# Decode beside a dense layer: a third key buffer, gathers one step ahead, and products of keys tied to the dense products

## The chip, the cores and the metric

One core of a Trainium2 chip runs the kernel in one launch. The metric is the device time of that launch in microseconds (us); the median of several runs counts. TensorE (PE) multiplies matrices, VectorE (DVE) and ScalarE (ACT) work on rows, GpSimd (POOL) gathers by index and does small operations, SyncE (SP) issues loads and stores.

## The reference

One layer of a decoder for a prompt of 512 tokens and, in the same launch, one new token for each of 8 sequences that have 4096 past tokens each. Both go through the same weights; the new tokens also read paged caches of keys and values (32 pages of 128 tokens, 8 heads of 64).

```python
h = rmsnorm(x, g_pre_mix)
qf, kf, vf, logf, qg, kg, vg, la, og, gfox, ggla = split(h @ w_in)
o_fox = softmax(q k^T / 8 + decay of the log forget gates, causal) @ v      # prompt
# new tokens, for each of 8 sequences:
lp = einsum('bqhd,bkhd->bhqk', q, k_past) * scale + suffix_sums(logf_past) + cn
ln = q . k_new * scale
p  = softmax over [lp, ln];  o_fox = p @ [v_past, v_new]
S_new, o_gla = gla(state, qg, kg, vg, la)                                   # chunks of 64
u = sigmoid(gfox) * (o_fox @ w_fox_out) + sigmoid(ggla) * (o_gla @ w_gla_out)
x = x + rmsnorm(u @ w_o)
x = x + rmsnorm(square(relu(rmsnorm(x) @ w_up)) @ w_down)
```

## The kernel before

**Dense work.** Everything is float32. A weight is loaded in pieces of 128x2x256 (`raw`, L234, on SP's queue) and split into a high part `wh` (a cast on ScalarE, L222) and a low part `wl` (a subtraction on VectorE, L223); the activations `h` and `c` are split likewise. A product of 256 columns is then three products per 128 rows of depth: high by high, high by low, low by high. Every product goes through the helper `mm` (L85), so its line is L85 whatever it computes; tiles tell them apart: `pmm` is dense work, `pdv` the value products of decode, `px` and `pd` smaller ones. The order in the code is: queries, the forget gates (`gates_small`: L372 to L379, a polynomial of ten steps on VectorE whose results are `lfs` for the new tokens and `lft` for the prompt; `lft` is transposed at L419), keys and values, the GLA projections, the output gates, the mix, w_o (`wo_fin` at L1181, once for each of four blocks of 128 rows: a sum of squares, a reciprocal root on GpSimd at L218, the residual sum at L1185, transposes at L324, and the split of the new `h` at L327 and L223), then the MLP.

**Decode.** `decode()` (L549) is a generator of steps (b, g): sequence b, group g of 16. `pump` (L643) is called between dense products and runs one step for every 3.1 us of dense work that has been written. A step gathers pages with `page_load` (L209, on GpSimd): `kk`, 512 KB of keys, 16 for a sequence, and `kv`, 1 MB of values, 8 for a sequence. `kk` and `kv` have two buffers each. A step multiplies keys by the query (L574) and reduces over the head (L575), both on VectorE, each in place or into `sc`. After the 16th step come the maximum (`mx`, L604 to L607), a transpose (L610), the common maximum (`dm`, L612 and L613), and the exponentials. While sequence b does its keys, TensorE multiplies the values of sequence b-1 (four `pdv` products for each `kv`).

**What sets the order.** The program is written in one order in Python; a scheduler that simulates a timeline then places each engine's instructions, by dependencies, buffers and the written order. Each engine runs its own list strictly in that order. A gather into `kk` waits for the reduction that last read its buffer, and one into `kv` for the last product that read it.

## Time and profile before

| | |
|---|---|
| median of three runs | 1068.25 us (1065.61 to 1074.95) |
| profiled execution | 1071.62 us |
| its span | 1069.9 us |
| mean granted TensorE clock | 0.956 |
| TensorE busy | 996.6 us, 93% |
| VectorE busy | 690.2 us, 65% |
| ScalarE busy | 427.3 us, 40% |
| GpSimd busy | 270.0 us, 25% |

The span is what the profiler saw, and the profiled execution is a run of its own beside the three. Busy time counts work, not waits; a TensorE that runs at half its clock counts as busy too, so its busy time is to be read with the granted clock. Decode runs from about 24 to 776 us of the span.

### The profile page before, as it was taken

What the parts mean: (1) busy time and instruction counts of PE and PEld (TensorE: products, weight loads), DVE (VectorE), ACT (ScalarE), POOL (GpSimd) and SP (SyncE); (2) the same over time, 40 slices, a digit from 0 to 9 for tenths busy, and PEclk for the clock granted to TensorE, in tenths of its full rate; (3) what the DMA queues carried; (4) which work ended last, traced back from release to release, by engine and by line L of the source; (5) the groups of instructions that cost most, each with busy time, mean ns of one, the idle gap of its engine ahead of it and who ended that gap; (6) DMA issues with size and microseconds to landing.
All of it is one profiled execution on the core that took longest, in us unless ns stands there. A gap on an engine that the chain in (4) does not pass through costs nothing.

```text
span 1069.9 us, 20743 instructions
## 1 busy us (share of the span) xinstructions
PE 996.6 (93%) x8183; PEld 830.5 (78%) x8183; DVE 690.2 (65%) x1238; ACT 427.3 (40%) x1110; POOL 270.0 (25%) x256
## 2 busy tenths in 40 slices
PE   7998999999999899999894799999999799999996
PEld 5987867867977787797784678788787588888995
DVE  8577766867989858887669779567333333233356
ACT  6424544534833414333233444336313453115442
POOL 5232243353342313423334333430100000000001
PEclk9997999999999979999896899999999899999999
DMA  6746788587578638966994687994667366677222
GB/s 194 251 143 197 272 299 286 182 314 276 169 284 292 190 103 266 310 222 205 343 346 154 232 318 240 330 335 142 222 229 237 120 205 214 213 237 235 81 76 86
DMA packets 134279, 242.03 MB, mean 226 GB/s; under 512 B 11627, under 2 KB 105150, under 8 KB 125990
## 3 DMA queue, kind: packets, MB, share of 16 engines
q0 software_dynamic: 28032, 135.28, 36.0%
q1 hardware_dynamic: 106150, 105.43, 31.0%
q8 instruction: 64, 1.05, 0.4%
q14 instruction: 33, 0.27, 0.1%
HBM read 235.14 MB, written 5.47 MB: 225 GB/s over the span
## 4 chain that ended last, share of the span: by engine, by line
PE 56%; DMA 21%; DVE 12%; issue 7%; POOL 2%; ACT 1%; DVEq 0%; POOLq 0%; SPq 0%; ACTq 0%
PE pmm L85 41%; DMA kk<-in_cache_k,ixki 14%; PE px L85 8%; PE pdv L85 4%; DVE kk L574 3%; DMA kv<-in_cache_v,ixvi 3%; DVE sc L575 3%; DVE wl L223 2%; DMA raw<-in_w_in 1%; PE pd L85 1%; DMA kv<-in_w_up 1%; DMA kv<-in_w_down 1%; POOL kk L209 1%; DMA c<-in_state_gla 1%; POOL kv L209 1%
## 5 line engine op out<-in xcount | busy, mean ns | idle before, releaser
L85 PE MATMUL pmm<-h,wh 128*128 128x256 f32 (+2 forms) x1696 | 360.7, 308 | 8.6 <-ACT h L222 4.1
L85 PEld LDWEIGHTS pmm<-h,wh 128*128 128x128 f32 x1696 | 279.9, 196 | 45.5 <-issue 16.9
L85 PE MATMUL pmm<-h,wl 128*128 128x256 f32 (+2 forms) x848 | 258.8, 307 | 0.0
L209 POOL DMA_INDIRECT kk<-in_cache_k,ixki x128 | 162.6, 1270 | 334.8 <-DVE sc L575 205.7
L85 PE MATMUL pmm<-wh,c 128*128 128x256 f32 x1280 | 233.9, 283 | 5.5 <-DVE c L1040 3.6
L85 PEld LDWEIGHTS pmm<-wh,c 128*128 128x128 f32 x1280 | 197.2, 190 | 27.4 <-issue 16.9
L223 DVE TENSOR_TENSOR wl<-raw,wh 128x512 fp32r<-128x512 f32 x240 | 161.7, 686 | 80.8 <-PE pmm L85 56.0
L574 DVE TENSOR_TENSOR kk<-kk,qb 128x1024 f32<-128x1024 f32 x128 | 156.2, 1221 | 83.7 <-DMA kk<-in_cache_k,ixki 81.9
L222 ACT CAST wh<-raw 128x512 fp32r<-128x512 f32 x240 | 146.7, 619 | 157.2 <-PE pmm L85 96.2
L85 PE MATMUL pmm<-wl,c 128*128 128x256 f32 x640 | 179.2, 282 | 1.1 <-DVE wl L223 1.1
L85 PEld LDWEIGHTS pmm<-h,wl 128*128 128x128 f32 x848 | 165.1, 195 | 11.4 <-issue 4.6
L575 DVE TENSOR_REDUCE sc<-kk 128x16 f32<-128x1024 f32 x128 | 154.7, 1211 | 0.7
L85 PEld LDWEIGHTS pmm<-wl,c 128*128 128x128 f32 x640 | 120.8, 190 | 9.8 <-issue 7.9
L209 POOL DMA_INDIRECT kv<-in_cache_v,ixvi x64 | 70.4, 1100 | 146.7 <-PE pdv L85 124.4
L218 POOL TENSOR_TENSOR rs<-rs,mhalf 128x1 f32<-128x1 f32 (+2 forms) x21 | 16.3, 776 | 292.8 <-DVE rs L217 290.8
L85 PE MATMUL pdv<-kv,pt 128*32 128x512 f32 x512 | 68.0, 612 | 8.6 <-DMA kv<-in_cache_v,ixvi 8.5
L85 PE MATMUL pmm<-wh,h 128*128 128x256 f32 x384 | 74.8, 287 | 0.0
L85 PEld LDWEIGHTS pmm<-wh,h 128*128 128x128 f32 x384 | 59.8, 188 | 4.8 <-issue 4.6
L85 PE MATMUL pmm<-wl,h 128*128 128x256 f32 x192 | 55.7, 291 | 0.3 <-DVE wl L223 0.3
L1339 DVE TENSOR_TENSOR c<-pmm,c 128x256 f32<-128x256 f32 x48 | 18.7, 421 | 57.4 <-PE pmm L85 57.0
L1293 DVE TENSOR_TENSOR c<-td,c 128x256 fp32r<-128x256 f32 (+1 forms) x50 | 24.8, 497 | 32.6 <-ACT td L1292 32.4
L85 PE MATMUL pmm<-c,wh 128*128 128x512 f32 x128 | 42.7, 418 | 1.6 <-DVE c L911 0.9
(335 smaller groups left out, 1099.5 us busy)
## 6 DMA issues: line engine op xcount, KB each, us to landing
raw<-in_w_in SPq DMA_DIRECT2D x80, 256.0 KB
raw<-in_w_up SPq DMA_DIRECT2D x64, 256.0 KB
raw<-in_w_down SPq DMA_DIRECT2D x64, 256.0 KB
kv<-in_w_down SPq DMA_DIRECT2D x24, 512.0 KB
kv<-in_w_up SPq DMA_DIRECT2D x18, 512.0 KB
raw<-in_w_o SPq DMA_DIRECT2D x16, 256.0 KB
kv<-in_w_o SPq DMA_DIRECT2D x8, 512.0 KB
c<-in_x_prompt SPq DMA_DIRECT2D x4, 512.0 KB
```

The costliest lines, as they stand in the source:

```text
L85: PE.matmul(out=out, lhsT=lhsT, rhs=rhs, start=start, stop=stop)
L209: G.indirect_dma_start(out=t, out_offset=None, in_=view, in_offset=bass.IndirectOffsetOnAxis(ap=ix[:, b, g:g + 1], axis=0))
L218: G.tensor_tensor(out=r, in0=a, in1=mhalf[:P, :n], op=ALU.pow)
L222: S.copy(out=hi, in_=raw)
L223: V.tensor_tensor(out=lo, in0=raw, in1=hi.bitcast(F32), op=ALU.subtract)
L574: V.tensor_tensor(out=K3, in0=K3, in1=qb[:, None, :].to_broadcast([128, KJ, 512]), op=ALU.mult)
L575: V.tensor_reduce(out=sc[:, g * 8 * KJ:(g + 1) * 8 * KJ], in_=K.rearrange("p (x d) -> p x d", d=64), axis=AX.X, op=ALU.add)
L1293: V.tensor_tensor(out=l, in0=r[:, 0:n], in1=d.bitcast(F32), op=ALU.subtract)
L1339: V.tensor_tensor(out=d, in0=p, in1=d, op=ALU.add)
```

## The change

`kk` gets a third buffer (BU), and the constant LK goes from 0 to 1, so that a step's code issues the gather of the next step's keys. `mm` remembers the last product that it issued (`last`). A step notes that product before its own work (`dense`), and `held` adds a dependency from it to the step's product of keys. All other code is the same; line numbers of the kernel after are higher by 1 from `mm` on and by 7 from `decode` on (L575 is L582).

```diff
--- before.py
+++ after.py
@@ -26,10 +26,10 @@
 TR = 544
 FP, LP, LQ = 3, 1, 1
 PA, PB, PC, PD, PE_ = 1, 1.2, 0.6, 0.6, 1
-LK, LV = 0, 2
+LK, LV = 1, 2
 TO = 1
 PF, PG, HN = 0.8, 1.5, 2
-BU = dict(h=4, c8=9, wh=6, wl=5, raw=5, kk=2, kv=2, td=2, ts=5, qb=2, tj=1, ev=1)
+BU = dict(h=4, c8=9, wh=6, wl=5, raw=5, kk=3, kv=2, td=2, ts=5, qb=2, tj=1, ev=1)
 PK = 2
 TAU = 3.1
 MS = 1
@@ -78,11 +78,12 @@
         return sb.tile(shape, dt, tag=name, name=f"{name}_{n_[0]}", bufs=bufs)
 
     clock = [0.0]
+    last = [None]
 
     def mm(out, lhsT, rhs, start, stop):
 
         clock[0] += np.prod(rhs.shape[1:]) * (4 if rhs.dtype == F32 else 1) / (4 if out.shape[0] == 32 else 1) / 2400
-        PE.matmul(out=out, lhsT=lhsT, rhs=rhs, start=start, stop=stop)
+        last[0] = PE.matmul(out=out, lhsT=lhsT, rhs=rhs, start=start, stop=stop)
 
 
     ptab = cst([32, 8], "ptab", I32)
@@ -546,6 +547,11 @@
     oS = cst([128, 4, 32], "oS")
     G.memset(oS, 0.0)
 
+    def held(ins, dense):
+
+        tc.add_manual_dep(ins.ins, dense.ins.name, mybir.DependencyInfo(
+            mybir.DependencyClass.Sync, mybir.DependencyReason.DATA), reason="a step of decode takes its turn")
+
     def decode():
         steps = [(b, g) for b in range(NB + 1) for g in range(NG)]
         pk, pv_ = [], []
@@ -560,6 +566,7 @@
                 pv_.append(page_load(vvw, ixvi, nv // NV, nv % NV, VJ, "kv"))
                 nv += 1
             K = pk.pop(0) if b < NB else None
+            dense = last[0]
             if g == 0:
                 if b < NB:
                     qb = new([128, 512], "qb")
@@ -571,7 +578,7 @@
                     pv = ps("dv")
             if b < NB:
                 K3 = K.rearrange("p (j x) -> p j x", j=KJ)
-                V.tensor_tensor(out=K3, in0=K3, in1=qb[:, None, :].to_broadcast([128, KJ, 512]), op=ALU.mult)
+                held(V.tensor_tensor(out=K3, in0=K3, in1=qb[:, None, :].to_broadcast([128, KJ, 512]), op=ALU.mult), dense)
                 V.tensor_reduce(out=sc[:, g * 8 * KJ:(g + 1) * 8 * KJ], in_=K.rearrange("p (x d) -> p x d", d=64),
                                 axis=AX.X, op=ALU.add)
             if b > 0:
```

The scheduler makes another order out of it. Ahead of the two places, the names: `kk` is a tile of keys and `qb` its query, `sc` the scores, `lf`, `lfs` and `lft` belong to the forget gates, `wl` is the low part of a weight; a number is a tile's own.

VectorE at the start, where the prompt's `lft` is finished, before:

```order
L379 SCALAR_TENSOR_TENSOR lfs<-lf_770,lf_772 8x8
L378 SCALAR_TENSOR_TENSOR lf_136_796<-lf_136_796,lf_135_795 128x32 x3
L574 TENSOR_TENSOR kk_939<-kk_939,qb_489 128x1024
L379 SCALAR_TENSOR_TENSOR lft<-lf_134_794,lf_136_796 128x32
L223 TENSOR_TENSOR wl_1051<-raw_1040,wh_1050 128x512
L575 TENSOR_REDUCE sc_491<-kk_939 128x16
L574 TENSOR_TENSOR kk_943<-kk_943,qb_489 128x1024
L541 COPY cn_1587<-pdv_1584 128x8
L423 SCALAR_TENSOR_TENSOR td_819<-ones,pd_812 8x512
L575 TENSOR_REDUCE sc_491<-kk_943 128x16
L223 TENSOR_TENSOR wl_1055<-raw_1042,wh_1054 128x512
```

and after:

```order
L542 COPY cn_1589<-pdv_1586 128x8
L611 TENSOR_TENSOR sc_493<-sc_493,bias_1581 128x256
L379 SCALAR_TENSOR_TENSOR lf_137_798<-lf_137_798,lf_136_797 128x32
L224 TENSOR_TENSOR wl_1061<-raw_1046,wh_1060 128x512
L613 TENSOR_REDUCE mx_1594<-sc_493 128x8
L380 SCALAR_TENSOR_TENSOR lft<-lf_135_796,lf_137_798 128x32
L534 SCALAR_TENSOR_TENSOR bias_1623<-rst,bias_1623 128x256
L614 TENSOR_TENSOR mx_1594<-mx_1594,cn_1589 128x8
```

Before, the tenth product of keys stands just ahead of `lft`, and six more of the first sequence follow it. After, `lft` stands behind all sixteen, the last of them five rows ahead of these, and behind the first two operations of the maximum (L611, L613).

GpSimd in the tail of w_o, before (`rs` at L218 or L219 is the reciprocal root of one row block, of which two blocks' stand ahead of these rows and the other two in them):

```order
L218 TENSOR_TENSOR rs_1176_6727<-rs_1175_6726,mhalf 128x1
L209 DMA kk_6915<-in_cache_k,ixki 128x1024
L209 DMA kk_6921<-in_cache_k,ixki 128x1024
L218 TENSOR_TENSOR rs_1189_6791<-rs_1188_6790,mhalf 128x1
L209 DMA kk_6989<-in_cache_k,ixki 128x1024
L209 DMA kv_6755<-in_cache_v,ixvi 128x2048
L209 DMA kv_6917<-in_cache_v,ixvi 128x2048
L209 DMA kk_6995<-in_cache_k,ixki 128x1024
L209 DMA kv_6991<-in_cache_v,ixvi 128x2048
L209 DMA kk_7003<-in_cache_k,ixki 128x1024
L209 DMA kk_7095<-in_cache_k,ixki 128x1024
```

and after:

```order
L210 DMA kv_6757<-in_cache_v,ixvi 128x2048
L210 DMA kv_6919<-in_cache_v,ixvi 128x2048
L210 DMA kk_6917<-in_cache_k,ixki 128x1024
L210 DMA kk_6923<-in_cache_k,ixki 128x1024
L210 DMA kv_6993<-in_cache_v,ixvi 128x2048
L219 TENSOR_TENSOR rs_1166_6671<-rs_1165_6670,mhalf 128x1
L210 DMA kv_7007<-in_cache_v,ixvi 128x2048
L219 TENSOR_TENSOR rs_1177_6729<-rs_1176_6728,mhalf 128x1
L210 DMA kv_7107<-in_cache_v,ixvi 128x2048
L219 TENSOR_TENSOR rs_1190_6793<-rs_1189_6792,mhalf 128x1
```

The value gathers have moved ahead of the roots: the last three roots of four stand behind `kv_6993`, `kv_7007` and `kv_7107`, where before all four stood ahead of `kv_6755`.

TensorE at the same place (`px` are the transposes of a row block, `pdv` from `kv` the value products), before:

```order
L85 MATMUL pmm_6885<-h_6049,wh_6565 128x256
L85 MATMUL pmm_6885<-h_6047,wl_6566 128x256
L85 MATMUL pdv_6542<-kv_6347,pt_6515 32x512 x4
L85 MATMUL pdv_6542<-kv_6527,pt_6515 32x512 x4
L324 MATMUL px_6795<-ident,c_1051_6043 128x128 x4
L324 MATMUL px_6804<-ident,c_1051_6043 128x128 x4
L85 MATMUL pdv_6542<-kv_6755,pt_6515 32x512 x4
```

and after:

```order
L325 MATMUL px_6609<-ident,c_1051_6043 128x128 x4
L325 MATMUL px_6618<-ident,c_1051_6043 128x128 x4
L86 MATMUL pdv_6544<-kv_6349,pt_6517 32x512 x4
L86 MATMUL pdv_6544<-kv_6529,pt_6517 32x512 x4
L86 MATMUL pdv_6544<-kv_6757,pt_6517 32x512 x4
L86 MATMUL pdv_6544<-kv_6919,pt_6517 32x512 x4
L325 MATMUL px_6675<-ident,c_1051_6043 128x128 x4
L325 MATMUL px_6684<-ident,c_1051_6043 128x128 x4
L86 MATMUL pmm_6857<-h_6048,wh_6555 128x256
```

The products of the first two value tiles stood just ahead of the fourth block's transposes (`px_6795`); they, and two more tiles, now stand between the first and the second block's (`px_6618` and `px_6675`).

## Rows read from the trace of the kernel before

**Rows 1.** The page: the chain that ended last, by line.
```profile
PE pmm L85 41%; DMA kk<-in_cache_k,ixki 14%; PE px L85 8%; PE pdv L85 4%; DVE kk L574 3%; DMA kv<-in_cache_v,ixvi 3%; DVE sc L575 3%; DVE wl L223 2%; DMA raw<-in_w_in 1%; PE pd L85 1%; DMA kv<-in_w_up 1%; DMA kv<-in_w_down 1%; POOL kk L209 1%; DMA c<-in_state_gla 1%; POOL kv L209 1%
```

**Rows 2.** Windows: span, then each engine's busy us (and instructions); granted clock; DMA share; GB/s.
```profile
75.00:100.00 25.00, 20.26 (x132) 16.50 (x131) 20.50 (x35) 7.81 (x20) 6.02 (x6) 0.73 0.60 183
375.00:400.00 25.00, 25.00 (x178) 22.32 (x176) 13.81 (x25) 5.07 (x14) 3.92 (x3) 0.77 0.34 109
400.00:500.00 100.00, 98.85 (x725) 82.75 (x726) 80.90 (x147) 34.90 (x107) 37.94 (x32) 0.97 0.77 255
500.00:525.00 25.00, 19.40 (x118) 14.52 (x118) 18.57 (x27) 7.32 (x24) 7.29 (x7) 0.86 0.78 297
567.00:612.00 45.00, 23.81 (x136) 18.91 (x135) 40.93 (x69) 16.34 (x44) 20.11 (x17) 0.70 0.60 191
612.00:700.00 88.00, 85.41 (x611) 69.71 (x610) 62.86 (x82) 35.27 (x84) 31.44 (x29) 1.00 0.86 302
776.00:1070.00 294.00, 275.87 (x2377) 237.08 (x2377) 110.01 (x250) 104.82 (x259) 5.36 (x8) 0.97 0.55 175
```

**Rows 3.** The page's groups: busy us, mean ns of one, then idle before and its releaser.
```profile
L209 POOL DMA_INDIRECT kk<-in_cache_k,ixki x128 | 162.6, 1270 | 334.8 <-DVE sc L575 205.7
...
L223 DVE TENSOR_TENSOR wl<-raw,wh 128x512 fp32r<-128x512 f32 x240 | 161.7, 686 | 80.8 <-PE pmm L85 56.0
L574 DVE TENSOR_TENSOR kk<-kk,qb 128x1024 f32<-128x1024 f32 x128 | 156.2, 1221 | 83.7 <-DMA kk<-in_cache_k,ixki 81.9
...
L575 DVE TENSOR_REDUCE sc<-kk 128x16 f32<-128x1024 f32 x128 | 154.7, 1211 | 0.7
...
L209 POOL DMA_INDIRECT kv<-in_cache_v,ixvi x64 | 70.4, 1100 | 146.7 <-PE pdv L85 124.4
L218 POOL TENSOR_TENSOR rs<-rs,mhalf 128x1 f32<-128x1 f32 (+2 forms) x21 | 16.3, 776 | 292.8 <-DVE rs L217 290.8
```

**Rows 4.** Timeline, GpSimd and VectorE, 51 to 56: start, us, work, idle time before it.
```profile
51.10 0.94 POOL L209 DMA_INDIRECT kk<-in_cache_k,ixki  x1 [7.37 <-DVE sc L575]
...
55.47 1.23 DVE L574 TENSOR_TENSOR kk<-kk,qb 128x1024 f32<-128x1024 f32 x1 [3.51 <-DMA kk<-in_cache_k,ixki]
```

**Rows 5.** Timeline of the start, VectorE and TensorE.
```profile
37.79 2.36 DVE L574 TENSOR_TENSOR kk<-kk,qb 128x1024 f32<-128x1024 f32 x2 [0.62 <-DMA qb<-qd]
...
78.27 0.18 DVE L379 SCALAR_TENSOR_TENSOR lft<-lf,lf 128x32 f32<-128x32 f32 x1
...
83.27 0.80 PE L85 MATMUL pmm<-h,wh 128*128 128x256 f32 x2 [2.94 <-ACT wh L222]
...
87.01 1.02 PE L85 MATMUL pd<-td,sel 128*8 128x256 f32 x2
```

**Rows 6.** Timeline, TensorE: the products with the GLA state.
```profile
370.56 5.73 PE L85 MATMUL px<-c,ts 64*32 64x128 f32 x32 [4.02 <-DMA c<-in_state_gla]
```

**Rows 7.** Timeline of the mix and of the tail of w_o, VectorE and TensorE.
```profile
499.40 1.22 DVE L574 TENSOR_TENSOR kk<-kk,qb 128x1024 f32<-128x1024 f32 x1 [4.07 <-DMA kk<-in_cache_k,ixki]
...
517.85 0.80 PE L85 MATMUL pmm<-wh,c 128*128 128x256 f32 x2 [3.37 <-DVE c L1040]
...
566.15 1.03 PE L324 MATMUL px<-ident,c 128*128 128x128 f32 x8
...
575.13 1.97 PE L324 MATMUL px<-ident,c 128*128 128x128 f32 x8 [7.11 <-DVE c L1185]
...
584.64 0.79 PE L85 MATMUL pmm<-h,wh 128*128 128x256 f32 x2 [4.12 <-ACT h L222]
...
605.23 1.94 PE L85 MATMUL pdv<-kv,pt 128*32 128x512 f32 x8 [5.69 <-DMA kv<-in_cache_v,ixvi]
```

**Rows 8.** The chain that ended last, 570 to 682: start, us, what.
```profile
573.88 1.20 DVE c L1185
...
597.96 5.14 DMA kv<-in_cache_v,ixvi
...
672.83 8.56 DMA kv<-in_cache_v,ixvi
```

## The prediction

> **What bounds the kernel now.** The list of engines says TensorE, busy nearly all the time, and the chain of waits is mostly its products, but 14% of that chain is the transfer of keys [rows 1]. So I read the windows next, stage by stage, and look for stretches where TensorE's busy time or its granted clock falls. It runs full after decode: in the last 294 us there is no key, and nothing that the change moves [rows 2]. The losses are at the start (75 to 100), around 375, at 500, and in the tail of the w_o product (567 to 612), where TensorE is busy 23.81 of 45 us and VectorE 40.93 [rows 2]. Then the engines' groups, for why keys wait. Each gather of keys waits on GpSimd for the reduction that frees its buffer (205.7 us in all) and each product waits for its gather on VectorE (81.9) [rows 3]. With two buffers a gather starts after the reduction two steps back, so only the work that VectorE has between that reduction and the product hides it. An early step shows it bare: gather issued at 51.10, product at 55.47 after 3.51 us of nothing [rows 4]. A value gather waits for TensorE instead (124.4) [rows 3].
>
> **What the third buffer gives.** The release moves from the reduction two steps back to three. Adding the durations of what stands between release and product in VectorE's order (a product 1.22, a reduction 1.21, a split 0.69 [rows 3]), I get a median of 5.4 us before and 8.5 after; 80 of 128 products have under 6 us before, 23 after. Most of the 81.9 us should go. But VectorE is no bound by itself, so the sum goes by where TensorE was held.
>
> **What the wait adds.** Each product may not start before the dense product issued ahead of its step. In the built order 29 of 128 products carry it as a wait of their own; in the rest an earlier wait covers it. Behind a held product VectorE's queue has weight splits that TensorE needs next, and GpSimd's has the gather that the reduction frees. By itself it costs 0 to 6, and I put it into the term for the middle below. Larger is what the scheduler makes of the new dependencies: steps come at other places among the splits.
>
> **Start: +8 (+5 to +14).** Before, 10 products stand ahead of the last step of the prompt's forget decay (lft); after, all 16 of the first batch do, and the batch's maximum too. VectorE's queue from the first product at 37.79 [rows 5] is then 16 × (1.22 + 1.21) = 38.9, 11 splits × 0.686 = 7.5, 26 short operations at about 0.15 (the row of lft has 0.18 [rows 5]) = 3.9, and the two of the maximum, at most a split each, 1.3: lft at 89.4 if VectorE never waits, against 78.27 before. Allowing for two or three of the old gather waits I take 92, and 95.5 for the maximum's way through TensorE and back (some 3 us of VectorE work stand in it). TensorE's queue needs both before its next products; before, it got to the same place at 87.0 [rows 5]. That is 8.5 later; 5 if the first waits vanish and the maximum overlaps, 14 with a lower clock after the stall, as 0.73 in this stretch already shows [rows 2]. A little is given back: the two outputs of the decay stand ahead of a weight's load before, and TensorE waits 2.94 for that weight at 83.27 [rows 5]; after, they stand behind it. I take 8.
>
> **GLA state: -10 (-12 to 0).** Before, 32 products wait 4.02 us for the state [rows 6], and the next 25 us run at 0.77 of the clock, (1 - 0.77) × 25 = 5.8 [rows 2]: 9.8 lost. After, they stand 96 dense products later, 96 × 0.116 = 11.1 us (2377 in 275.87 at the end [rows 2]). The load moves too, behind two weights and a query, which I put at 5 to 7 us. The rest, 4 to 6, just covers the wait.
>
> **Middle, 400 to 566: +3 (0 to +6).** Products of keys stand 4 to 9 splits earlier, so 8 to 17 us more VectorE work lies ahead of the splits that TensorE takes. VectorE is busy 80.90 of 100 there [rows 2], so it is 89 to 98 of 100 if the idle time, much of it for keys, goes. It fits, barely, and with the hold above I take 3.
>
> **Mix, 500 to 525: -5 (-9 to 0).** VectorE waits 4.07 us for keys at 499.40, and TensorE then 3.37 for its sum at 517.85 [rows 7]. The stretch misses 25 - 19.40 = 5.6 plus about 3.5 of clock at 0.86 [rows 2]. After, these products have 9 to 17 us between release and product in place of 4 to 7. I take just over half of 9.1, since the extra work ahead slows the same engine.
>
> **Tail of w_o: -8 (-16 to +4).** From the first row block's transposes (566.15) to the end of the value products at 605.23 + 1.94 it takes 41.0 us, with TensorE waiting 7.11 for the residual sum, 4.12 for the split activation and 5.69 for values [rows 7]. VectorE's order has nine products of keys there before, and about four after; five pairs of 2.43 would free 12 us. But GpSimd's order puts the second reciprocal root behind a value gather which waits for the value product ahead of it, and the others behind one gather more each. I walk that chain from the first transposes, 2.0 for eight [rows 7]: the products of two value tiles, 2 × 0.97 [rows 7]; a gather, 1.10 to issue [rows 3] and 5.1 to 8.6 to land (the chain has 5.14 and 8.56 [rows 8]); a tile's products and another issue, 2.1; the root 0.78 [rows 3], the sum 1.20 [rows 8], transposes 2.0, the activation 3 to 4 (4.12 before), 24 products at half rate, 24 × 2 × 0.116 = 5.6, then transposes, a tile, an issue, root and sum 6.0, and the last transposes 2.0. That is 33 to 37, with 2 to 4 for one more gather 35 to 41, against 41. In it TensorE does the products of five value tiles more, 4.9, which it need not do later: a gain of 5 to 11, and I take 8. If each of three gathers holds it for 3 us more than that, it is a loss of 4 (41 + 9 - 41 - 4.9); if VectorE alone was the limit, a gain of 12 + 4.9, some 16.
>
> **Other waits, 612 to 735: -2 (-4 to +3).** TensorE is busy 85.41 of 88 us there [rows 2], so there is little to gain, and 302 GB/s are moving already: earlier gathers may delay weights.
>
> **Sum.** 8 - 10 + 3 - 5 - 8 - 2 = -14, against the profiled execution's 1071.62: 1057.6. That execution was 3.4 above the median of the runs shown, so I forecast **1054**.
>
> **A rule of the skill, weighed.** The first gather shown took 4.37 us from issue to its product [rows 4], value gathers up to 8.56 [rows 8]. The Trainium skill, "DMA: Bandwidth & Descriptors", section "Anatomy of one DMA — SWDGE (gpsimd) path", puts such a transfer at 2.0 us plus its bytes at 436 GB/s; for 512 KB that is an estimate of 3.2 us. By that rule most key gathers would already be hidden behind the 5.4 us of VectorE work, and the sum would be 1061 in place of 1054, the last rival below. The trace disagrees: 4.37 us for this gather, with VectorE idle for 3.51 of them [rows 4].
>
> **Rivals.**
> *Slower: VectorE becomes the bound.* Place: the start and 400 to 566. If VectorE's idle time doesn't shrink there, the 8 to 17 us of moved work delay the splits one for one: +16 in place of +3, +14 at the start, nothing at the mix or after 612, the state's 10 and 4 of the tail: 14 + 16 - 10 - 4 = +16, or 1084. It decides from the point where start and middle hold back over 25 us, what the other terms give. For it: VectorE has 19.1 us free in 100 there [rows 2] and takes up to 17. Against it: 81.9 us of key waits [rows 3] are what makes much of that idle. Chance 0.18.
> *No change.* The waits removed lay beside TensorE's work, and value gathers pace the tail. Start +8, state -5, middle +3, mix -3, tail 0, other -1: +2, or 1070. For it: TensorE's own waits were for sums, values and activations, none for keys. Chance 0.25.
> *The change doesn't do what it says.* GpSimd runs in order, and a key gather issued ahead stands behind value gathers that wait for TensorE (124.4 us [rows 3]); the third buffer stays empty and the key waits stay. Then only the order counts: +8 - 10 + 3 - 4 = -3, or 1065. Against it: 205.7 us of GpSimd's waits are for reductions of keys [rows 3]. Chance 0.05.
> *Gathers are hidden already.* If a gather lands within the 5.4 us of VectorE work, a third buffer removes nothing; mix and other go to 0: -7, or 1061. [rows 4] and the 81.9 us speak against it. Chance 0.03.
>
> **How the numbers follow.** The forecast has 0.49, with its own range of 1043 to 1064; a measurement of this kernel can't tell less than about 1% from no change, so faster is below 1057.6 and slower above 1078.9. Of the forecast's 0.49, 0.38 lies below and 0.11 between. Of the 0.33 of no change and the two small rivals 0.06 falls below (the tail's or the mix's gain comes all the same), 0.02 above (the start at +14), and 0.25 between. The slower rival's 0.18 lies above. So 0.44, 0.36 and 0.20. The range drops the ends of the slower rival and of the forecast's lucky side: 1039 to 1081.
>
> **What would show it.** Right: the wait of key products on their gathers falls under 40 us; TensorE reaches the products behind the first batch's maximum some 8 us later than before; no wait for the state; fewer than 6 products of keys between the first and last residual sum. Wrong: splits awaited by TensorE between 400 and 566 (VectorE as the bound); TensorE waiting over 8 us for values in the tail; key waits near 80 us. What breaks the forecast most easily is the start, as its stall is worked out from an order, and the tail, where two gathers stand in series.

## The result and the profile after

The changed kernel takes 1083.51 us (median of four runs, 1079.69 to 1087.73), beside 1071.60 for the kernel before in the same session: a ratio of 1.012 with an interval of 1.0077 to 1.0162. It is slower by about 1.2%, where 1054 was forecast, and lies above the range. The profiled execution took 1080.65, with a span of 1078.9 (before 1069.9). Here and below a ratio leaves out single executions that ran clearly slower than the others of their kernel (one of 1110.51 with the wait alone, one of 1063.60 with ten steps); the medians count them.

The page of the kernel after, the chain that ended last, by line:

```profile
PE pmm L86 53%; PE px L86 10%; PE pdv L86 6%; DMA kv<-in_cache_v,ixvi 6%; DMA kk<-in_cache_k,ixki 3%; DVE kk L581 2%; PE pd L86 1%; DVE sc L582 1%; DMA kv<-in_w_down 1%; POOL kk L210 1%; DMA raw<-in_w_in 1%; PE px L692 1%; DMA kv<-in_w_up 1%; DVE wl L224 1%; DMA kv<-in_w_o 1%
```

The transfer of keys, 14% of the chain in [rows 1], is down to 3%. The groups of the same page say the same of the waits (busy us, mean ns of one, idle time before and its releaser):

```profile
L210 POOL DMA_INDIRECT kk<-in_cache_k,ixki x128 | 175.7, 1373 | 318.1 <-DVE sc L582 237.1
L224 DVE TENSOR_TENSOR wl<-raw,wh 128x512 fp32r<-128x512 f32 x240 | 162.8, 687 | 83.7 <-PE pmm L86 56.4
L581 DVE TENSOR_TENSOR kk<-kk,qb 128x1024 f32<-128x1024 f32 x128 | 155.6, 1221 | 61.5 <-DMA kk<-in_cache_k,ixki 43.2
...
L210 POOL DMA_INDIRECT kv<-in_cache_v,ixvi x64 | 76.3, 1192 | 150.3 <-PE pdv L86 134.7
```

Products of keys wait 43.2 us for their gathers in place of 81.9 [rows 3]. So the buffer does what it is for, and the kernel is slower all the same. The windows of the kernel after, with the columns of [rows 2], show where:

```profile
75.00:100.00 25.00, 13.82 (x85) 10.26 (x83) 19.65 (x39) 2.30 (x4) 10.35 (x7) 0.66 0.60 192
400.00:500.00 100.00, 81.25 (x574) 61.14 (x571) 77.58 (x141) 29.20 (x106) 35.71 (x33) 0.88 0.67 224
420.00:430.00 10.00, 2.72 (x17) 0.72 (x12) 6.02 (x13) 0.93 (x6) 3.88 (x5) 0.71 0.95 333
430.00:440.00 10.00, 5.65 (x32) 3.31 (x32) 8.40 (x14) 1.58 (x7) 5.84 (x5) 0.78 1.05 375
500.00:525.00 25.00, 25.00 (x200) 20.86 (x200) 17.19 (x24) 8.45 (x20) 13.65 (x9) 1.00 0.91 331
776.00:1070.00 294.00, 284.96 (x2459) 243.31 (x2457) 108.68 (x248) 105.78 (x259) 5.75 (x8) 0.99 0.55 175
```

From 400 to 500 TensorE is busy 81.25 us where it was 98.85 [rows 2], and from 420 to 430 only 2.72 of 10. VectorE is not fuller there: 77.58 of 100, before 80.90 [rows 2].

Windows at fixed times mislead once two kernels are shifted against each other, so I worked out a table by TensorE's own order. The trace has the same 5280 dense records (`pmm`) in both kernels. Between the n-th and a later one, I take the time that passed and subtract what all of TensorE's records in between take at the high clock (0.1165 us for a dense record of 256 columns, 0.124 for a record of a value product, 0.02 to 0.23 for the small ones). What is left is time that TensorE lost to waits or to a low clock (to rounding, the differences of 8.5 and the 0.7 by which the first record starts later are the 9.0 by which the span grew):

```
dense records      starts at        lost, us        predicted
                 before  after   before  after  diff   term
 329- 941 start    62.8   63.2     20.5   30.4   +9.9    +8
 941-1552         205.5  218.6     17.2   20.3   +3.1     -
1552-1717 state   360.8  372.9     16.2    1.3  -14.9   -10
1717-1929 middle  410.8  404.6      7.2   35.2  +28.0    +3
1929-2493 mix     466.9  493.7     12.0    5.8   -6.2    -5
2493-2705 tail    561.0  581.5     27.0   19.5   -7.5    -8
2705-3528         624.8  640.5      7.5    4.9   -2.6    -2
the rest                           13.7   12.4   -1.3     -
```

Five terms of the prediction are near what happened; together they are -21.3 where -17 was forecast. The term for the middle is wrong by 25, where the whole sum is wrong by 23 (+9.0 in place of -14). The split between two of the rows depends on the prices: 64 small products of the state's update moved from the state's stretch into the middle, and with all small records at their mean distance at the high clock (0.067 us for these) the state gains 12.8 and the middle loses 25.8. The sum of the two stays.

**What happens in the middle.** The timeline of the kernel after, SyncE, TensorE and ScalarE (start, us, work, idle time before it):

```profile
381.31 0.85 SPq L930 DMA_DIRECT2D c<-in_state_gla  x1
...
409.16 0.28 PE L86 MATMUL pmm<-h,wl 128*128 128x256 f32 x1
...
425.24 0.38 SPq L985 DMA_DIRECT2D out_gla_state_sample<-c  x1
...
427.17 1.93 PE L86 MATMUL pdv<-kv,pt 128*32 128x512 f32 x8 [6.38 <-DMA kv<-in_cache_v,ixvi]
430.45 1.94 PE L86 MATMUL pdv<-kv,pt 128*32 128x512 f32 x8 [1.35 <-DMA kv<-in_cache_v,ixvi]
...
435.72 0.28 ACT L346 ACTIVATE tj<-px 128x128 bf16<-128x128 f32 x1 [14.73 <-PE px L86]
...
440.35 0.39 ACT L1013 ACTIVATE c<-pmm 128x256 f32<-128x256 f32 x1 [3.03 <-DVE c L918]
...
440.79 0.51 PE L86 MATMUL pmm<-h,wh 128*128 128x264 f32 x2 [4.25 <-ACT c L1013]
```

From 409.44 to 440.79 TensorE does no dense product at all, only decode's and the GLA's small ones. The dense products have filled the PSUM banks that the code gives them (three), and the first evacuation, the gate's tanh on ScalarE (L1013), runs at 440.35. Two things stand ahead of it. Its output is a new 1 MB tile in the pool `c8`, which has nine buffers, and the one that it gets is that of the new tokens' GLA state: the state must be loaded (381.31), used, updated by VectorE between products of keys, and stored (issued at 425.24). And it stands in ScalarE's list behind the sums of squares of a GLA chunk (L346 at 435.72), whose chain runs through all four engines, with value tiles that wait for gathers interposed on TensorE (427.17, 430.45) and products of keys on VectorE.

The store came last. ScalarE has done its part of the chunk at 437.32 and is then idle for 3.03 us. The profile puts this wait down to VectorE's L918, which ends at 440.05. But the kernel before runs the same operation (L911, at 423.49) after the tanh (L1006, at 422.65), so the tanh does not need it. What ScalarE's sequencer waits for, 3.78 us from 436.53, are two DMA queues; the newest transfer on one is the state's load, on the other its store, whose last completions in the trace come at 440.06, 440.14 and 440.28, 15.0 us after its issue:

```profile
L1013 ACTq EVENT_SEMAPHORE  x1: 3782/3782/3782, 436.5 to 436.5; - x1
```

The same places before:

```profile
361.49 0.86 SPq L923 DMA_DIRECT2D c<-in_state_gla  x1
...
409.22 0.38 SPq L978 DMA_DIRECT2D out_gla_state_sample<-c  x1
...
422.65 0.39 ACT L1006 ACTIVATE c<-pmm 128x256 f32<-128x256 f32 x1
423.09 0.51 PE L85 MATMUL pmm<-h,wh 128*128 128x264 f32 x2
```

Before, the load stands 20 us earlier and the store 16, and TensorE reaches the stop later in its own work: it ran dense products until 418.08 and has none for 5.0 us, until 423.09. The change put the load 20 us later and took away the wait at the state's products, so TensorE reaches the stop 9 us earlier and the state's store comes later. What was gained at the state is paid back in the next stretch.

**A second stop.** The middle has one more, after the 1872nd dense record, where TensorE waits for the row norm of the next chunk (L911 on VectorE). VectorE, after:

```profile
469.09 2.36 DVE L581 TENSOR_TENSOR kk<-kk,qb 128x1024 f32<-128x1024 f32 x2
...
471.97 0.17 DVE L218 TENSOR_SCALAR rs<-ssg 128x4 f32<-128x4 f32 x1
...
474.34 1.22 DVE L582 TENSOR_REDUCE sc<-kk 128x16 f32<-128x1024 f32 x1
475.59 1.13 DVE L911 SCALAR_TENSOR_TENSOR ts<-px,rs,c 128x128 f32<-128x128 f32 x4
```

TensorE at the same place, and the window around it (columns as in [rows 2]):

```profile
476.09 1.16 PE L915 MATMUL px<-ident,ts 128*128 128x128 f32 x4 [4.29 <-DVE ts L911]
```

```profile
470.00:480.00 10.00, 4.13 (x28) 3.13 (x21) 9.74 (x23) 2.07 (x6) 5.77 (x6) 0.77 0.84 270
```

VectorE is full here (9.74 of 10), and two products and two reductions of keys stand ahead of the norm and of its input (L218). In the kernel before TensorE's longest wait in this part of the middle is 0.94 us. With the prices by mean distance, the middle loses 17.6 up to the 1752nd record and 13.8 behind it, where it lost 1.0 and 4.6 before.

The value waits in TensorE's list of waits tell of decode's new place too (us in all, times, longest), after:

```profile
PE pdv L86 <- DMA kv<-in_cache_v,ixvi: 24.3, 10, 7.9
PE pmm L86 <- DVE wl L224: 6.4, 4, 2.9
```

and before:

```profile
PE pdv L85 <- DMA kv<-in_cache_v,ixvi: 8.5, 4, 5.7
```

### The profile page after: what moved, and what is told of

Same layout as the page of the kernel before. It is cut to its first block, busy times and chain, and to the rows that moved or that the text cites. A ratio compares the mean times of both kernels' runs of the same rounds, so it can differ in the third digit from the quotient of the medians.

```text
span 1078.9 us, 20775 instructions
## 1 busy us (share of the span) xinstructions
PE 995.2 (92%) x8183; PEld 821.3 (76%) x8183; DVE 692.6 (64%) x1238; ACT 427.6 (40%) x1110; POOL 289.2 (27%) x256
## 4 chain that ended last, share of the span: by engine, by line
PE 73%; DMA 12%; DVE 7%; issue 4%; POOL 2%; ACT 1%; POOLq 0%; SPq 0%; DVEq 0%; ACTq 0%
PE pmm L86 53%; PE px L86 10%; PE pdv L86 6%; DMA kv<-in_cache_v,ixvi 6%; DMA kk<-in_cache_k,ixki 3%; DVE kk L581 2%; PE pd L86 1%; DVE sc L582 1%; DMA kv<-in_w_down 1%; POOL kk L210 1%; DMA raw<-in_w_in 1%; PE px L692 1%; DMA kv<-in_w_up 1%; DVE wl L224 1%; DMA kv<-in_w_o 1%
## 5 line engine op out<-in xcount | busy, mean ns | idle before, releaser
L86 PE MATMUL pmm<-h,wh 128*128 128x256 f32 (+2 forms) x1696 | 356.1, 306 | 11.8 <-ACT c L1013 4.3
L86 PEld LDWEIGHTS pmm<-h,wh 128*128 128x128 f32 x1696 | 275.9, 193 | 45.4 <-issue 17.5
L210 POOL DMA_INDIRECT kk<-in_cache_k,ixki x128 | 175.7, 1373 | 318.1 <-DVE sc L582 237.1
L581 DVE TENSOR_TENSOR kk<-kk,qb 128x1024 f32<-128x1024 f32 x128 | 155.6, 1221 | 61.5 <-DMA kk<-in_cache_k,ixki 43.2
L582 DVE TENSOR_REDUCE sc<-kk 128x16 f32<-128x1024 f32 x128 | 154.5, 1213 | 0.6
L210 POOL DMA_INDIRECT kv<-in_cache_v,ixvi x64 | 76.3, 1192 | 150.3 <-PE pdv L86 134.7
L86 PE MATMUL pdv<-kv,pt 128*32 128x512 f32 x512 | 76.9, 645 | 25.6 <-DMA kv<-in_cache_v,ixvi 24.3
L219 POOL TENSOR_TENSOR rs<-rs,mhalf 128x1 f32<-128x1 f32 (+2 forms) x21 | 16.2, 772 | 300.9 <-DVE rs L218 299.4
L86 PEld LDWEIGHTS pdv<-kv,pt 128*32 128x32 f32 x512 | 12.0, 111 | 45.6 <-DMA kv<-in_cache_v,ixvi 30.4
L1300 DVE TENSOR_TENSOR c<-td,c 128x256 fp32r<-128x256 f32 (+1 forms) x50 | 24.7, 498 | 31.7 <-ACT td L1299 29.2
```

Source lines behind the costliest of these rows:

```text
L86: last[0] = PE.matmul(out=out, lhsT=lhsT, rhs=rhs, start=start, stop=stop)
L210: G.indirect_dma_start(out=t, out_offset=None, in_=view, in_offset=bass.IndirectOffsetOnAxis(ap=ix[:, b, g:g + 1], axis=0))
L219: G.tensor_tensor(out=r, in0=a, in1=mhalf[:P, :n], op=ALU.pow)
L581: held(V.tensor_tensor(out=K3, in0=K3, in1=qb[:, None, :].to_broadcast([128, KJ, 512]), op=ALU.mult), dense)
L582: V.tensor_reduce(out=sc[:, g * 8 * KJ:(g + 1) * 8 * KJ], in_=K.rearrange("p (x d) -> p x d", d=64), axis=AX.X, op=ALU.add)
L1300: V.tensor_tensor(out=l, in0=r[:, 0:n], in1=d.bitcast(F32), op=ALU.subtract)
```

## The experiments

The theory with which I began: the third buffer makes the scheduler place decode's steps ahead of the dense work (start, middle), and the wait restrains that a little. The rival: the wait is what costs, and the buffer by itself would help. They are A and B in the expectations; the later theories V, G, S and M are told where each first stands, and these count the middle from the 1752nd to the 1968th dense record. All edits are to the kernel after unless another is named. Each table entry below is the time lost as above, and each ratio is against the kernel before in the same session. A row is one profiled execution. "Same order" is the kernel after with LK at 0: all its engines have the same orders, and its entries differ from those of the kernel after by up to 3.8 us, so smaller differences between rows say nothing.

```
lost, us         start  middle  state  mix  tail  the rest   median us
before            20.5     7.2   16.2  12.0  27.0   13.7     1071.60
after             30.4    35.2    1.3   5.8  19.5   12.4     1083.51
same order (LK)   29.9    38.7    1.3   5.8  17.2   16.2     1086.94
buffer alone      41.1    31.5    4.8   2.9  21.3   12.5     1096.59
wait alone        28.8    15.0    8.0   8.1  21.8   40.1     1102.42
ten steps early    9.2    21.2    3.6  17.1  10.7   13.3     1051.56
fewer values      29.9    37.4    1.3   6.1  19.4   13.1     1081.68
fewer keys        31.0    23.0    2.0   6.1  17.8   13.7     1066.28
store in pieces   31.0    39.0    1.3   6.0  18.7   12.3     1087.94
state in pieces   30.2    22.3   -1.1   7.9  18.3   12.8     1070.01
```

The middle's two stops apart, with the small products at their mean distance (so the two add up to 2 to 4 less than above):

```
lost, us              1717-1752   1752-1929
before                      1.0         4.6
after                      17.6        13.8
same order (LK)            20.2        14.6
ten steps early             4.3        15.3
fewer values               20.2        13.9
fewer keys                 16.8         3.6
state in pieces             8.4        10.4
pieces, fewer keys          9.8         4.1
```

**The buffer alone.**

```diff
-LK, LV = 1, 2
+LK, LV = 0, 2
...
-                held(V.tensor_tensor(out=K3, in0=K3, in1=qb[:, None, :].to_broadcast([128, KJ, 512]), op=ALU.mult), dense)
+                V.tensor_tensor(out=K3, in0=K3, in1=qb[:, None, :].to_broadcast([128, KJ, 512]), op=ALU.mult)
```

> Third buffer alone, without the wait. Theory A (the third buffer lets the order run decode ahead, and the losses at the start and between 400 and 490 come from that order; the wait only restrains it): 18 products of keys stand ahead of lft, so the start loses 10 us or more, value tiles bunch even more in the middle (four of them at one place), and the time is 1085 to 1110 us; waits of key products for gathers under 60 us. Theory B (the wait on the dense product is what costs, the third buffer helps): no loss in the middle, 1050 to 1066 us.

1096.59 us (1089.66 to 1098.17), ratio 1.0236 (1.0177 to 1.0296): slower than with the wait. Key waits fall to 43.7. In the order 18 products of keys stand ahead of `lft` (10 before, 16 after). The start loses 41.1 and the middle 31.5, so both losses come with the buffer. The wait alone has a part of them too (28.8 and 15.0, next run).

**The wait alone.**

```diff
-LK, LV = 1, 2
+LK, LV = 0, 2
...
-BU = dict(h=4, c8=9, wh=6, wl=5, raw=5, kk=3, kv=2, td=2, ts=5, qb=2, tj=1, ev=1)
+BU = dict(h=4, c8=9, wh=6, wl=5, raw=5, kk=2, kv=2, td=2, ts=5, qb=2, tj=1, ev=1)
```

> The wait alone, with two buffers and no gather ahead. Theory A: the start is as before (10 products ahead of lft), the middle loses under 5 us, key waits stay at 70 to 90 us, and the time is 1060 to 1076 us. Theory B: products of keys wait over 30 us for dense products, and the time is 1080 us or more.

1102.42 us (1091.05 to 1110.51), ratio 1.0267 (1.0188 to 1.0347), the slowest of all. Theory A had it near the kernel before. Theory B had 1080 us or more, but by products of keys that wait over 30 us for dense products, and the trace has no such wait. The profiled execution took 1110.51, so its rows are read for places, not for sizes. Key waits are 112.7. In its order the last value tile stands behind 3845 of the 5280 dense records (before behind 3571, after 3519, with the buffer alone 3429): decode ends later, and the new tokens' w_o and MLP, which need it, run with little dense work beside them. The windows of that kernel, and its timeline of TensorE:

```profile
860.00:880.00 20.00, 8.82 (x50) 1.36 (x46) 1.88 (x5) 4.43 (x12) 0.56 (x1) 0.50 0.53 170
```

```profile
884.86 1.02 PE L340 MATMUL pd<-ident,qb 8*128 8x8 f32 x8 [8.71 <-DVE qb L337]
```

So neither part helps by itself: the buffer runs decode early, the wait runs it late, and together they partly cancel.

**The gather one step ahead taken away** (LK alone).

```diff
-LK, LV = 1, 2
+LK, LV = 0, 2
```

> The kernel after with the gather in its own step again (LK = 0). The order of every engine is built the same as with LK = 1, so both theories expect the time of the kernel after within 0.5%, 1079 to 1088 us, and the waits for keys at about 43 us. If issuing the gather a step ahead mattered by itself, the time would differ by over 1%.

1086.94 us (1081.25 to 1090.24), ratio 1.014 (1.0089 to 1.0192), as the kernel after. Key waits are 36.5, where about 43 was expected. The orders of all engines are the same row for row with LK at 0 and at 1: the scheduler places a gather by its buffer, not by the step in which it is written. "A gather one step ahead" is the third buffer's doing; LK does nothing here.

**Ten steps before the first scores.** `pump` lets up to 16 steps run before the first batch has its scores; here ten.

```diff
-        while owed[0] >= 1 and (scored[0] or count[0] < NG):
+        while owed[0] >= 1 and (scored[0] or count[0] < 10):
```

> The kernel after, but only 10 steps in place of 16 may be written before the new tokens' scores exist, so that 10 products stand ahead of lft as before the change. Theory A: TensorE gets back 8 to 13 us by the 528th dense product, the middle keeps a loss of 10 to 25, since five value tiles stand at one place there too: 1066 to 1078 us. Theory B: within 4 us of the kernel after, 1080 to 1088.

1051.56 us (1047.58 to 1063.60), ratio 0.9808 (0.9751 to 0.9865): faster than both kernels, and by far more than expected. The windows of that kernel:

```profile
75.00:100.00 25.00, 25.00 (x220) 23.11 (x219) 9.72 (x22) 13.27 (x38) 0.00 (x0) 1.00 0.39 120
400.00:500.00 100.00, 90.54 (x617) 73.14 (x616) 87.66 (x138) 34.54 (x102) 42.59 (x33) 0.95 0.77 270
```

With ten products ahead of `lft`, the stall at the start is gone (25.00 of 25, before 20.26 [rows 2]); the start loses 9.2, less than the 20.5 before with the same ten ahead. The state's store is issued at 389.77, 35 us earlier than after, and TensorE waits 0.30 for the evacuation. The middle still loses 21.2, 14 more than before, most of it at the second stop, where TensorE waits 5.08 us for the row norm at 438.75. The tail loses 10.7.

For the middle the next theories were the value tiles that TensorE waits for, and VectorE's work on keys in the GLA's chain.

**Fewer value tiles.** Six of the eight value tiles of the fourth sequence are neither gathered nor multiplied.

```diff
-                pv_.append(page_load(vvw, ixvi, nv // NV, nv % NV, VJ, "kv"))
+                pv_.append(None if nv // NV == 3 and 0 < nv % NV < 7 else page_load(vvw, ixvi, nv // NV, nv % NV, VJ, "kv"))
...
-                    for j in range(VJ):
+                    skip = b == 4 and 0 < g // 2 < 7
+                    for j in range(0 if skip else VJ):
```

> The kernel after, with the gathers and products of six of the eight value tiles of the fourth sequence left out (so that sequence's result is not computed in full); these are the tiles that stand bunched between the 1752nd and 1871st dense product. The order of VectorE is unchanged up to there. Lost time of TensorE from the 1752nd to the 1968th dense product: 33 us in the kernel after, 5 before. Theory V (TensorE stands behind bunched value tiles, for which two buffers are too few): 17 or less, and the whole 18 to 30 us shorter, 1054 to 1066 us (6 of it are the products left out). Theory G (the GLA chain between TensorE, VectorE and ScalarE stands behind products of keys): 26 to 34 are left, and the whole is 1074 to 1080 us.

1081.68 us, ratio 1.0097 (1.0060 to 1.0135); the middle loses 37.4. The theory of the value tiles falls: the wait only changes its name. TensorE's timeline in that kernel, then VectorE's:

```profile
434.77 0.45 PE L916 MATMUL px<-ident,ts 128*128 128x128 f32 x1 [11.02 <-DVE ts L912]
...
429.17 1.23 DVE L581 TENSOR_TENSOR kk<-kk,qb 128x1024 f32<-128x1024 f32 x1 [5.03 <-DMA kk<-in_cache_k,ixki]
```

VectorE now stands 5.03 us before a product of keys, with the GLA's row norm (L912), for which TensorE waits, behind it.

**Fewer products of keys.** Fifteen of the sixteen products and reductions of the fifth sequence are left out.

```diff
+                    if b == 4:
+                        V.memset(sc, 0.0)
...
-            if b < NB:
+            if b < NB and not (b == 4 and g > 0):
```

> The kernel after, with 15 of the 16 products and reductions of keys of the fifth sequence left out (its scores are zeros there); they run on VectorE in the same stretch. The value tiles then stand at eight different places instead of four at one. Theory V and theory G both expect the stretch from the 1752nd to the 1968th dense product to lose under 12 us; V because the tiles are apart, G because the chain finds VectorE free. 1055 to 1068 us. If it still loses over 20, both are wrong and the dense products themselves were placed too late.

1066.28 us (eight runs, 1060.04 to 1072.54), ratio 0.9942 (0.9911 to 0.9974); the middle loses 23.0, 12.2 less than after. What holds the evacuation now is bare. The timeline of that kernel, ScalarE and TensorE:

```profile
441.44 0.38 ACT L1015 ACTIVATE c<-pmm 128x256 f32<-128x256 f32 x1 [6.02 <-DMA out_gla_state_sample<-c]
441.87 0.81 PE L86 MATMUL pmm<-h,wh 128*128 128x264 f32 x2 [7.29 <-ACT c L1015]
```

The store was issued at 424.20, and its buffer came free 17.2 us later: with the keys' work gone, the state's buffer alone holds the gate until 441.4, and the first stop loses as much as after (16.8, after 17.6). What the keys' work costs is the second stop, which falls from 13.8 to 3.6.

**The value products tied too**, each tile's to the dense product of its step.

```diff
+                        if j == 0:
+                            held(last[0], dense)
```

> The kernel after, where value products too wait for the dense product ahead of their step. In the built order six value tiles now stand at the 1752nd dense product in place of four, with the keys' order unchanged there; in the tail of w_o the tiles stand one by one. Theory V: the stretch from 1752 to 1968 loses 40 to 50 us, the tail 5 less than in the kernel after: 1086 to 1098 us. Theory G: the stretch loses 28 to 36, the whole 1076 to 1084 us.

1082.64 us, ratio 1.0106 (1.0066 to 1.0147); the middle loses 39.2. No change that shows.

**Ten steps, and the value products tied.**

```diff
-        while owed[0] >= 1 and (scored[0] or count[0] < NG):
+        while owed[0] >= 1 and (scored[0] or count[0] < 10):
...
+                        if j == 0:
+                            held(last[0], dense)
```

> First sequence limited to 10 early steps, and value products tied to their turn as well. Its order is that of the run with 10 early steps up to the tail of w_o, where the value tiles stand one by one (at 2592, 2640, 2688 and so on) instead of in pairs. Theory V expects the tail to lose 3 to 6 us less than with 10 early steps alone, 1045 to 1052 us; if values don't pace the tail, it is the same within 3 us, 1050 to 1055.

1060.06 us (1057.15 to 1065.27), ratio 0.9887 (0.9854 to 0.9920), slower than with ten steps alone. The tail loses 11.4 (10.7), but the stretch behind it 18.0 (7.4).

**The state's store in pieces.** The update writes into small tiles, each stored by itself, so that the state's own buffer is free without a store.

```diff
+            so = new([128, 4, 128], "ts")
...
-                    V.scalar_tensor_tensor(out=S0[:, bi * 2 + hp, :], in0=S0[:, bi * 2 + hp, :],
+                    V.scalar_tensor_tensor(out=so[:, b * 2 + hp, :], in0=S0[:, bi * 2 + hp, :],
...
+            nc.sync.dma_start(out=so_v[:, 4 * b4:4 * b4 + 4, :], in_=so)
```

> The kernel after, with the updated GLA state of the new tokens written to small tiles and stored in four pieces of 256 KB, so that the 1 MB buffer of the state, which the first gate product of the second gate needs, is free when VectorE has done the update, and not only when a store of 1 MB has landed (issued at 425.24, first evacuation into the buffer at 440.35 in the kernel after). Theory S (dense products stand still between 409 and 441 for that buffer: state load, state products, update, store): the stretch from the 1752nd to the 1968th dense product loses 15 to 24 us in place of 33, the whole 1068 to 1078. Theory V (bunched value tiles): all eight tiles now stand at one place, so it loses 40 or more, 1090 or more. Theory G: 30 to 36, unchanged time.

1087.94 us (1085.70 to 1089.62), ratio 1.0167 (1.0096 to 1.0239); the middle loses 39.0. Theory S missed and theory V was near (40 or more lost, 1090 us or more): the store's landing is not the one thing, and TensorE now meets waits for values instead. Its timeline in that kernel:

```profile
420.51 1.94 PE L86 MATMUL pdv<-kv,pt 128*32 128x512 f32 x8 [5.90 <-DMA kv<-in_cache_v,ixvi]
```

**The same edit in the kernel before** (as there, with `so` in place of `S0`).

```diff
+            so = new([128, 4, 128], "ts")
...
+            nc.sync.dma_start(out=so_v[:, 4 * b4:4 * b4 + 4, :], in_=so)
```

> The same edit of the state's store in the kernel before. Theory S: the stretch lost only 5 us there, so at most 4 us are gained: 1064 to 1074 us. Theory V: six tiles are closer together, 2 to 8 us slower.

1076.62 us (ten runs), ratio 1.0069 (1.0031 to 1.0107), inside theory V's 2 to 8 us more; the middle loses 19.3 where the kernel before loses 7.2. A loss of 12 in the middle can be had without the change, by another order alone.

**The same edit with ten steps.**

```diff
-        while owed[0] >= 1 and (scored[0] or count[0] < NG):
+        while owed[0] >= 1 and (scored[0] or count[0] < 10):
...
+            so = new([128, 4, 128], "ts")
```

> The same edit in the kernel with 10 early steps, which lost 19 us in the stretch. Theory S: 6 to 12 us less, 1040 to 1048 us against the 1051.6 without it. Theory V: four value tiles in a row where there were three: 2 to 6 us slower. Theory G: unchanged.

1062.30 us, ratio 0.9932 (0.9898 to 0.9967); the middle loses 28.4 (21.2 with ten steps alone). No help.

**The whole state in pieces**: load, products, update and store of two sequences at a time, in small tiles; no 1 MB buffer for it at all.

```diff
-        S0 = c8(shape=[128, 16, 128])
-        nc.sync.dma_start(out=S0, in_=I["state_gla"].rearrange("o b (a e) k v -> (o e k) (b a) v", e=2))
...
+        for b4 in range(4):
+            S0 = new([128, 4, 128], "ts")
+            nc.sync.dma_start(out=S0, in_=s_in[:, 4 * b4:4 * b4 + 4, :])
...
+            nc.sync.dma_start(out=s_out[:, 4 * b4:4 * b4 + 4, :], in_=S0)
+            yield
```

> The kernel after, with the new tokens' GLA state handled in four pieces of 256 KB (load, products, update, store) in small tiles, so that it takes no 1 MB buffer. In the built order the update's products now stand between dense products ahead of the 1752nd, and the gate's first evacuation waits for no buffer. Theory S (the late chain of the state alone holds the dense products): the stretch from 1752 to 1968 loses 8 to 16 us in place of 33, 1062 to 1071 us. Theory M (three things end at the same place, about 440: the store's landing, value tiles that wait for gathers on TensorE, and key products ahead of the GLA chain on VectorE; taking one away shows the next): 20 to 28 are lost, 1070 to 1080 us.

1070.01 us (ten runs, 1063.85 to 1078.44), ratio 1.0007 (0.9972 to 1.0043): the whole slowdown is given back, at the short end of theory M's 1070 to 1080. The middle loses 22.3 in place of 35.2, most of the difference at the first stop (8.4 in place of 17.6). The first evacuation of the gate in that kernel:

```profile
433.14 0.39 ACT L1014 ACTIVATE c<-pmm 128x256 f32<-128x256 f32 x1
```

It waits for nothing of its own, and stands 7.2 us earlier than after.

**The state in pieces, and fewer values; then fewer keys** (with the edits shown above, and the same work left out).

```diff
-                    for j in range(VJ):
+                    for j in range(0 if skip else VJ):
```

> State in pieces, and the six value tiles of the fourth sequence left out as before. Theory M: two of three causes are gone, and the stretch loses 10 to 20; VectorE's key products ahead of the GLA chain remain, TensorE waits for the state of the GLA chunk (its normalised rows) on VectorE. Theory S: no change from the state in pieces alone beyond 4 us.

1070.68 us, ratio 1.0022 (0.9983 to 1.0061); the middle loses 28.8, no less than with the values. Missed.

```diff
-            if b < NB:
+            if b < NB and not (b == 4 and g > 0):
```

> State in pieces, and 15 of 16 products of keys of the fifth sequence left out as before; the value tiles are spread in this order. Theory M: all three causes are gone, and the stretch loses under 10 us, near the 5 of the kernel before. Theory S: the same as the state in pieces alone within 4 us. If it still loses over 15, a fourth cause is at work.

1059.78 us, ratio 0.9933 (0.9902 to 0.9964); the middle loses 15.7. Better by 6.6 than the state in pieces alone, but not below ten as expected: 8.5 over the kernel before stay, all at the first stop (9.8). In this kernel TensorE waits there for the row norm of the new tokens' state, and VectorE for its reciprocal root (L219), which GpSimd reaches at 418.74, behind six gathers:

```profile
419.35 0.35 DVE L984 SCALAR_TENSOR_TENSOR ts<-ts,rs,ts 128x128 f32<-128x128 f32 x1 [8.79 <-POOL rs L219]
```

```profile
419.85 0.45 PE L986 MATMUL px<-ident,ts 128*128 128x128 f32 x1 [5.58 <-DVE ts L984]
```

**The state in pieces, and ten steps.**

```diff
-        while owed[0] >= 1 and (scored[0] or count[0] < NG):
+        while owed[0] >= 1 and (scored[0] or count[0] < 10):
```

> State in pieces with 10 early steps, which alone gave 1051.6 us with 19 lost in the stretch. Theory S: 5 to 10 lost, 1040 to 1046 us. Theory M: four value tiles stand in a row at the 1872nd product, so 14 to 22 stay, 1046 to 1054 us.

1063.70 us, ratio 0.9958 (0.9924 to 0.9991): slower than ten steps alone; the middle loses 31.7. Where the state comes early, as with ten steps, its one buffer doesn't hold the gate (0.30 us), and the pieces have nothing to free. What in the new order costs the 10 us is not shown. The fastest kernel of the study stays the one with ten steps: 1051.56.

## Why the prediction was wrong

**The step that failed is "Middle, 400 to 566: +3 (0 to +6)".** It measured +28.0. The step asked one question of this stretch: whether VectorE can deliver the splits in time with 8 to 17 us more work ahead of them. It can: TensorE waits for splits 6.4 us in the whole span, all of it before 94 us. (How 4 to 9 splits make 8 to 17 us is not worked out in the step either.) But TensorE wasn't held by splits. At the first stop it was held by PSUM banks that nobody emptied, because the evacuation stood behind the GLA chunk's chain and, last, the state's buffer. At the second it was held by a row norm behind VectorE's products of keys. [rows 6] already had the state's load as the end of a wait; I took its removal as pure gain and priced the load at "behind two weights and a query", 5 to 7 us. It moved by 20, and I did not ask who else needs the buffer into which the state is loaded.

How it divides, by the split above: 16.6 more at the first stop and 9.2 more at the second. Taking the state out of the large buffer gives back 9.2 at the first and 3.4 at the second. Leaving out the fifth sequence's products of keys gives back 10.2 at the second and nothing that shows at the first. Both together bring the second to its level before (4.1 and 4.6) and leave 8.8 at the first. These 8.8 have no cause shown in the kernel after: the wait for the state's row norm, found in the kernel with both edits, is 0.20 us there. Value tiles left out alone give nothing. That an order alone can cost such a sum is shown by the kernel before with its store in pieces (7.2 to 19.3).

**The others, point by point.**
- Start, +8: +9.9. `lft` came at 94.00 (worked out: 92) and the common maximum at 97.36 (95.5), by the timeline of VectorE after:

```profile
94.00 0.17 DVE L380 SCALAR_TENSOR_TENSOR lft<-lf,lf 128x32 f32<-128x32 f32 x1
...
97.36 0.21 DVE L620 TENSOR_SCALAR dm<-ident,m 8x8 f32<-8x8 f32 x1
```

The walk through the built order held to 2 us. The ten-step kernel, with six products fewer ahead of `lft`, loses 9.2 there in place of 30.4.
- State, -10 (-12 to 0): -14.9 (-12.8 with the small products at their mean distance), a little beyond its bound; no wait for the state is left. (The products with the state are 64; [rows 6] shows the first group of 32.)
- Mix, -5: -6.2. TensorE's wait for its sum is gone (no wait over 0.4 us from 493.7 to 581.5), and the window is full (25.00 of 25, [rows 2] 19.40). VectorE still waits once for keys, 4.14 us at 514.91, without holding TensorE.
- Tail, -8: -7.5. The mechanism was right in both halves: two products of keys stand between the first and the last residual sum (under six foretold), and TensorE waits for values longer, 12.8 us in the tail. I had set over 8 there as a sign that I was wrong; the stretch still lost 7.5 less. (The step's best case, 12 + 4.9, is 17 and not 16.) TensorE's timeline after, in the tail:

```profile
599.24 1.93 PE L86 MATMUL pdv<-kv,pt 128*32 128x512 f32 x8 [7.90 <-DMA kv<-in_cache_v,ixvi]
...
604.39 1.97 PE L325 MATMUL px<-ident,c 128*128 128x128 f32 x8 [0.29 <-DVE c L1192]
```

- Other waits, -2: -2.6.
- Key waits under 40: 43.2, just over, and 36.5 in the same order with LK at 0.

**The rivals.** The slower one gave 1084, and 1083.5 was measured. That is luck: it wanted VectorE as the bound from 400 to 566, splits delayed and nothing gained at the mix. VectorE's busy share fell from 80.90 to 77.58 of 100, key waits halved, no split was awaited there, and the mix gained 6.2. Of its place it had the middle right, and at the second stop the engine too: there VectorE is full, and its products of keys stand in front of a row norm, not of splits (the 10.2 above). "The change doesn't do what it says" holds for LK alone. "Gathers are hidden already" falls with the 38.7 us of key waits that went.

With the middle at its forecast the profiled execution would have been 1080.65 - 25 = 1055.7, beside the 1057.6 worked out: no other step was off by more than 5. The 3.1 lost from the 941st to the 1552nd record had no term.

## What to carry to other kernels

A wait that a change removes at one place leaves the engine early at the next: for each such gain, ask which resource that the removed wait was filling stops the engine next, and count PSUM banks and shared buffers as well as engines. Where a load is moved, follow its buffer to whoever gets it next, to the landing of the last store out of it. And where a scheduler orders the work, a buffer is also a permission to run ahead: a limit on how far (ten steps in place of sixteen) was worth 32 us here, where the buffer and the wait had cost 12. The limit was not run in the kernel before, nor with the buffer or the wait alone, so how much of the gain needs them is not shown.

## What the runs showed of the hardware

A 1 MB store of state gave its buffer free 17.2 us after SyncE issued it with fewer keys (424.20 to 441.44), while the transfers moved 349 to 376 GB/s. By its last completion it took 15.0 us in the kernel after (425.24 to 440.28, at 333 to 375 GB/s), 11.5 with fewer values and 16.6 with the value products tied. Value gathers made TensorE wait up to 6.38 us in the middle of the kernel after and 7.90 in its tail. TensorE's clock falls where it waits: 0.66 at the start, 0.71 from 420 to 430. It is then late for its own small work as well: eight records of a value tile take 1.93 us at 427.17, after 6.38 us of waiting and at a granted clock of 0.50 (1.2 GHz), and 1.07 in the kernel with the state in pieces at 426.42, after 0.74 us and at 1.00 (2.4 GHz):

```profile
426.42 1.07 PE L86 MATMUL pdv<-kv,pt 128*32 128x512 f32 x8 [0.74 <-DMA kv<-in_cache_v,ixvi]
```

GpSimd's waits for reductions of keys say little about the waits that count: they are 205.7 us before [rows 3], 237.1 after, 178.5 with the buffer alone and 224.8 with the wait alone, while VectorE's products wait 81.9, 43.2, 43.7 and 112.7 for their gathers.
